# A second buffer for one weight block of every second column pair, and two of its down tiles moved to the end

## The chip, the cores and the metric

The kernel runs on one core of one Trainium2 chip. The core has a matrix engine (TensorE, PE in the rows; its weight loads are PEld), a vector engine (VectorE, DVE), an activation engine (ScalarE, ACT), GpSimd (POOL) and SyncE (SP), which only issues transfers. All five take their instructions in order and wait for one another through semaphores. The metric is the time of one execution on the device in microseconds (us), the median of several runs.

## The reference

One block of a streaming encoder on 512 positions of width 2048, all in float32: a mixer (a gated linear recurrence beside a banded attention) and then a gated feed-forward part with a causal depthwise convolution of width 3. The change touches the feed-forward part:

```
h2 = rms_norm(x, g_ffn[l])
up = causal_dwconv(h2 @ w_up[l], conv_w[l], conv_b[l])      # 2048 -> 2 * 5632
a, gate = jnp.split(up, 2, axis=-1)
x = x + (a * jax.nn.silu(gate)) @ w_down[l]                 # 5632 -> 2048
```

## The kernel before

**Up-projection.** The 11264 columns of `w_up` are taken as 44 pairs of 128 (128 columns of `a` with their 128 of the gate). The first four pairs (`lead`) are computed directly. Pairs 4 to 43, called units here, use a Strassen-Winograd scheme: the weights of a unit are four blocks of 128x1024 (512 KB each), and seven products of weight combinations with activation combinations give the result. `unit_loads` fetches what a unit needs into four buffers of the pool `ur`: `s1` (a sum of two blocks, the second added by an accumulating transfer that GpSimd issues), `a22`, `a11` and `a12`. A fifth tile, `s3`, goes into the fixed buffer `spare`. In the order of the products: `a22` (product T4), `a11` (B11), `s1` (T1), S2 = `s1`+`a11`, added in place into `a11` at L935 (T2), `a12` (B21), S4 = `a11`+`a12`, added in place into `a12` at L939 (B22), and `s3` (T3). Each is split into two float16 parts (`split16`: ACT at L880, then DVE at L881), into one of six buffers `whl`, and a product is 24 matmuls of 256 columns on these and on the split activations `thi`, `tlo`.

**Scales.** Before the first split of a unit its scale must be known: ACT takes the absolute sums of the four blocks and of the unit's down tiles (L886, into a throw-away tile `junk`), DVE and ACT make a diagonal `dg` (L770), a small matmul spreads the maximum over all partitions (L772), and DVE inverts it. One call of `period_scales` serves a unit and the down tiles that stand beside it. `m_scale` does the same for a group of four results.

**Down-projection.** It has 11 groups of four pairs with 8 weight tiles each, 88 down tiles in all, taken from `queue` in order. A down tile is a 512 KB load into one of three buffers `raw`, a split, 24 matmuls of 512 columns and two additions into the accumulators (L1063). Units 5 and 6 have three down tiles beside them, units 7 to 43 two each, unit 4 none; the last 8 tiles run in pairs after unit 43 (`plan_downs`), each pair with a scale of its own.

**Order.** `take(3)` writes out the splits up to three operands ahead of the product or down tile that consumes one; whatever a split needs first (the scale of the next unit, the loads of its down tiles) is written out there too. So with two down tiles the scale of unit j+1 is written out just before the last product T3 of unit j; with three it is written out only at the first down tile of unit j, after the code that follows T3 (the sums into `z`, the convolution taps, the gate). `unit_loads(j+1)` stands behind the addition S4 of unit j. The tile framework keeps this as a priority, moves an instruction forward when its inputs and a buffer are free, and gives a pool's buffers out in the order of the requests; so a load is issued when the tile that held its buffer has had its last reader.

**The buffers of `act`.** The pool `act` has 48 buffers of 2 KB. In `lead` it holds the 32 tiles of the split activations `hh`, `hl_`, and `t_prep(0)` to `t_prep(7)` put the 32 tiles of `thi`, `tlo` there; in the second half of `lead` each step i frees four of the former.

Of the kernel before, what the change touches and what calls it, by code (L numbers as in the profile page):

```python
# [8 lines left out]
F32 = mybir.dt.float32  # L9
# [5 lines left out]
ALU = mybir.AluOpType  # L15
PSUM = bass.MemoryType.PSUM

P = 128
T = 512
# [4 lines left out]
NPAIR_FF = 44  # L24
N_WARM = 12
NGRP = 11
N_LEAD = 4
H = 256
# [3 lines left out]
N_DOWN = N_MIX + 16 + 4 * (NPAIR_FF - N_LEAD)  # L32
# [20 lines left out]
def block_kernel(ctx: ExitStack, tc: tile.TileContext, xT, wst, cols, bias_t, masks, yT):  # L53
# [3 lines left out]
    cst = ctx.enter_context(tc.tile_pool(name="cst", bufs=1))  # L57
    wp = ctx.enter_context(tc.tile_pool(name="wp", bufs=3))
    actp = ctx.enter_context(tc.tile_pool(name="actp", bufs=48))
# [11 lines left out]
    def nm(s):  # L71
        cnt[0] += 1
        return f"{s}{cnt[0]}"
# [4 lines left out]
    def vo_t():  # L78
        return vop.tile([P, T], F32, tag="vo", name=nm("vo"))
# [7 lines left out]
    def mm_t():  # L87
        return ps_mm.tile([P, T], F32, tag="mm", name=nm("mm"))
# [4 lines left out]
    V = nc.vector  # L93
    A = nc.scalar
# [3 lines left out]
    def c3(ap, n):  # L98
        return ap.rearrange("p (a b) -> p a b", a=n)
# [25 lines left out]
    def next_w():  # L125
        while len(wq) < 1 + LOOK and wstate["prep"] < wstate["end"]:
            prep_w()
        return wq.pop(0)
# [81 lines left out]
    def rstd(r, ms):  # L210

        A.activation(r, ms, AF.Ln, bias=epst)
        A.activation(r, r, AF.Exp, scale=-0.5)
        t = wk_t()[:, :r.shape[1]]
        V.scalar_tensor_tensor(out=t, in0=ms, scalar=EPS, in1=r, op0=ALU.add, op1=ALU.mult)
        V.scalar_tensor_tensor(out=t, in0=t, scalar=-0.5, in1=r, op0=ALU.mult, op1=ALU.mult)
        V.scalar_tensor_tensor(out=r, in0=t, scalar=1.5, in1=r, op0=ALU.add, op1=ALU.mult)
# [37 lines left out]


    ssq = vo_t()
    R1 = cst.tile([P, T], F32, name="R1")
    r1c = cst.tile([P, NT], F32, name="r1c")

    def split(src):
# [14 lines left out]
    def finish_r1():  # L276
# [5 lines left out]
        rstd(r1c, ps2[:, 0:NT])  # L282
        rstd(R1, ps)

# [73 lines left out]
    def evict_r1(ps, alloc):  # L358
        x = alloc()
        V.tensor_tensor(out=x, in0=ps, in1=R1, op=ALU.mult)  # L360
        return x
# [299 lines left out]
    for blk in range(2):  # L661
# [3 lines left out]
        for h in range(4 * blk, 4 * blk + 4):  # L665
# [7 lines left out]
            g = hg_mixer(h, vt, pf, pq, pg)  # L673
            next(g)
            gens.append(g)
    for blk in range(2):
        vt = v_evict(v_gemm())
        for h in range(4 * blk, 4 * blk + 4):
# [3 lines left out]
            g = at_mixer(h, vt, pq, pk, bt)  # L682
# [4 lines left out]
    acc = [None] * KT  # L687
# [45 lines left out]
    zp = ctx.enter_context(tc.tile_pool(name="zp", bufs=1))  # L733
# [14 lines left out]

    R2 = R1

# [30 lines left out]
    gs = cst.tile([P, KT], F32, name="gs")  # L781
# [12 lines left out]
    thi, tlo = [None] * 8, [None] * 8  # L794

    def t_prep(i):
        z = zp.tile([P, 8, H], F32, tag="z", name=nm("z"))
        c2 = lambda ap: ap.rearrange("p (a b) -> p a b", a=2)
        V.scalar_tensor_tensor(out=z[:, 0:8:7, :], in0=c2(acc[i][:, :]), scalar=gs[:, i:i + 1], in1=c2(R2[:, :]), op0=ALU.mult, op1=ALU.mult)
        V.scalar_tensor_tensor(out=z[:, 1:3, :], in0=c2(acc[i + 8][:, :]), scalar=gs[:, i + 8:i + 9], in1=c2(R2[:, :]), op0=ALU.mult, op1=ALU.mult)  # L800
        b11, b21, b22, t1, t2, t3, t4, b12 = [z[:, j, :] for j in range(8)]
        V.tensor_tensor(out=t1, in0=b11, in1=b12, op=ALU.subtract)
        V.scalar_tensor_tensor(out=t2, in0=t1, scalar=-1.0, in1=b22, op0=ALU.mult, op1=ALU.subtract)
        V.tensor_tensor(out=t3, in0=b22, in1=b12, op=ALU.subtract)
        V.scalar_tensor_tensor(out=t4, in0=t2, scalar=-1.0, in1=b21, op0=ALU.mult, op1=ALU.subtract)
        hs, ls = [], []
        for o, n in ((0, 4), (4, 3)):
            h = actp.tile([P, n, H], F16, tag="act", name=nm("th"))
            l = actp.tile([P, n, H], F16, tag="act", name=nm("tl"))
            A.copy(out=h, in_=z[:, o:o + n, :])  # L810
            V.tensor_tensor(out=l, in0=z[:, o:o + n, :], in1=h, op=ALU.subtract)
            hs += [h[:, j, :] for j in range(n)]
            ls += [l[:, j, :] for j in range(n)]
        thi[i], tlo[i] = hs, ls
# [45 lines left out]
    def ur_t():  # L860
        return urp.tile([P, 1024], F32, tag="ur", name=nm("ur"))

    def raw_t():
        return wp.tile([P, 1024], F32, tag="raw", name=nm("raw"))

    def load(t, i):
        nc.sync.dma_start(out=t, in_=wst[i])
        return t

    def load_sum(t, i, k):  # L870
        nc.sync.dma_start(out=t, in_=wst[i])
        nc.gpsimd.dma_start(out=t, in_=wst[k], accum_op=ALU.add)
        return t
# [12 lines left out]
            A.activation(junk_t(), t, AF.Abs, accum_out=r[:, k:k + 1])  # L886

    units = {}

    def unit_loads(j):  # L890
        u = units.setdefault(j, {})
        i = N_MIX + 16 + 4 * (j - N_LEAD)
        u["s1"] = load_sum(ur_t(), i + 2, i + 3)
        u["a22"] = load(ur_t(), i + 3)
        u["a11"] = load(ur_t(), i)
        u["a12"] = load(ur_t(), i + 1)

    def down_loads(ds):
        return [load(raw_t(), N_DOWN + 8 * g + c2) for g, c2 in ds]

    def period_scales(j, ds):

# [63 lines left out]
    def product(ps, b):  # L966
        t = take(3)
        for k in range(8):
            cs = slice(k * P, (k + 1) * P)
            cl = slice(1024 + k * P, 1024 + (k + 1) * P)  # L970
            mm3(ps, t[:, cs], t[:, cl], thi[k][b], tlo[k][b], k == 0, k == 7)
        if later:
            later.pop(0)()

    def up_unit(j):
        bank = [mm_t() for _ in range(4)]
        z = zp.tile([P, 8, H], F32, tag="z", name=nm("z"))
        s1, u2, v = z[:, 7, :], z[:, 4, :], z[:, 5:7, :]
        two = lambda ap: ap.unsqueeze(1).broadcast_to([P, 2, H])
        b = lambda i: c3(bank[i], 2)  # L980
        product(bank[3][:, H:], T4)
        product(bank[0][:, 0:H], B11)
        A.copy(out=s1, in_=bank[0][:, 0:H])
        product(bank[2][:, 0:H], T1)
        product(bank[1][:, H:], T2)
        product(bank[1][:, 0:H], B21)
        V.tensor_tensor(out=z[:, 0:5:4, :], in0=b(1), in1=two(s1), op=ALU.add)
        product(bank[3][:, 0:H], B22)
        product(bank[2][:, H:], T3)
        V.tensor_tensor(out=v, in0=b(2), in1=two(u2), op=ALU.add)  # L990
        V.tensor_tensor(out=z[:, 1:3, :], in0=b(3), in1=v, op=ALU.add)
        V.tensor_tensor(out=z[:, 3, :], in0=bank[2][:, H:], in1=v[:, 0, :], op=ALU.add)
        cw = units.pop(j)["cw"]
        zf = z.rearrange("p a b -> p (a b)")
        ya = taps(zf[:, 0:T], j, cw[:, 0])
        yg = taps(zf[:, T:2 * T], NPAIR_FF + j, cw[:, 1])
        gated(j, ya, yg, zf[:, 0:T])
# [11 lines left out]
    def lead():  # L1009
        half = N_LEAD // 2  # L1010
        n = 0
        for j in range(half):
            u = c3(ur_t(), 2)
            for e in range(2):
                ps = mm_t()
                for h in range(2):
                    wh, wl = next_w()
                    for k in range(8):
                        cs = slice(k * P, (k + 1) * P)
                        kt = 8 * h + k  # L1020
                        mm3(ps, wh[:, cs], wl[:, cs], hh[kt], hl_[kt], kt == 0, kt == KT - 1)
                        if n == 0 and k == 3:
                            finish_r2()
                    if n % 2 == 1:
                        t_prep(n // 2)
                    n += 1
                evict_r2(ps, u[:, e])
            lead_taps(j, [u[:, 0], u[:, 1]], (ssa, rmask)[j])
        unit_loads(N_LEAD)
        pss = [mm_t() for _ in range(2 * half)]  # L1030
        for i in range(8):
            wh, wl = next_w()
            for e, kt in enumerate((i, i + 8)):
                for c in range(2 * half):
                    cs = slice((4 * e + c) * P, (4 * e + c + 1) * P)
                    mm3(pss[c], wh[:, cs], wl[:, cs], hh[kt], hl_[kt], i + e == 0, i + e == 8)
            if i % 2 == 1:
                t_prep(4 + i // 2)
            if i == 4:
                period_scales(N_LEAD, [])  # L1040
        us = [evict_r2(ps, actp.tile([P, T], F32, tag="act", name=nm("u"))) for ps in pss]
        later.extend([lambda j=j: lead_taps(half + j, us[2 * j:2 * j + 2]) for j in range(half)])
# [23 lines left out]

    mrp = ctx.enter_context(tc.tile_pool(name="mrp", bufs=2))
    steps = []
    queue = [(g, c2) for g in range(NGRP) for c2 in range(8)]
    done = 0  # L1070
    for j in range(N_LEAD, NPAIR_FF):
        steps.append(j)
        n = 0 if j == 4 else 3 if j < 7 else 2
        ds = queue[done:done + n]
        done += n
        plan_unit(j, ds)
        steps += ds
# [8 lines left out]
    for st in steps:  # L1086
# [8 lines left out]
        elif st % 4 == 3:  # L1095
            g = st // 4
# [129 lines left out]
```

## Time and profile before

| what | value |
|---|---|
| median of 3 runs | 2345.21 us (2338.12 to 2345.74) |
| the profiled execution, its own time | 2340.17 us |
| its span, first to last instruction | 2338.3 us |
| mean granted TensorE clock | 0.986 |
| TensorE matmul busy | 2210.7 us, 95% of the span |
| VectorE busy | 1672.2 us, 72% |
| ScalarE busy | 1334.9 us, 57% |
| transfers | 294.21 MB, mean 126 GB/s |

The profile is of one execution. Busy times count the engine's own instructions; matmuls are pipelined and their ends modelled. "Idle before" an instruction is time in which its engine did nothing, followed by what ended that time. The granted clock is a share of 2.4 GHz.

### The profile page before, as it was taken

What the parts mean: (1) busy time and instruction counts of PE and PEld (TensorE: products, weight loads), DVE (VectorE), ACT (ScalarE), POOL (GpSimd) and SP (SyncE); (2) the same over time, 40 slices, a digit from 0 to 9 for tenths busy, and PEclk for the clock granted to TensorE, in tenths of its full rate; (3) what the DMA queues carried; (4) which work ended last, traced back from release to release, by engine and by line L of the source; (5) the groups of instructions that cost most, each with busy time, mean ns of one, the idle gap of its engine ahead of it and who ended that gap; (6) DMA issues with size and microseconds to landing.
All of it is one profiled execution on the core that took longest, in us unless ns stands there. A gap on an engine that the chain in (4) does not pass through costs nothing.

```text
span 2338.3 us, 34658 instructions
## 1 busy us (share of the span) xinstructions
PE 2210.7 (95%) x13666; PEld 1698.5 (73%) x13666; DVE 1672.2 (72%) x2669; ACT 1334.9 (57%) x2110; POOL 271.0 (12%) x261
## 2 busy tenths in 40 slices
PE   9999999999999999986799999999999999999989
PEld 7888887888888887874467676666777676666664
DVE  7678568758568645975477877777777787777774
ACT  5455445445355334564566667666767676666652
POOL 4223123300001112000000000000000000000001
PEclk9999999999999999997899999999999999999999
DMA  6222222222323422444355555555555655555532
GB/s 206 90 73 73 90 72 81 79 93 82 99 87 97 142 99 91 142 123 128 103 160 154 150 152 148 158 154 162 154 162 154 162 153 149 152 144 158 157 100 99
DMA packets 82755, 294.21 MB, mean 126 GB/s; under 512 B 9568, under 2 KB 10208, under 8 KB 82592
## 3 DMA queue, kind: packets, MB, share of 16 engines
q1 hardware_dynamic: 68112, 240.34, 31.1%
q0 software_dynamic: 14480, 51.65, 12.0%
q8 instruction: 107, 1.75, 0.3%
q14 instruction: 56, 0.46, 0.1%
HBM read 287.76 MB, written 4.19 MB: 125 GB/s over the span
## 4 chain that ended last, share of the span: by engine, by line
PE 42%; DVE 22%; ACT 16%; DMA 14%; issue 5%; POOL 0%; SPq 0%; ACTq 0%; POOLq 0%; DVEq 0%
DMA ur<-wst 13%; PE mm L131 10%; PE mm L133 10%; PE mm L132 10%; ACT junk L886 8%; DVE whl L881 7%; ACT whl L880 3%; PE mx L131 2%; PE mx L133 2%; PE mx L132 2%; DVE vo L1063 2%; DVE vo L819 2%; ACT dg L770 1%; ACT mhl L847 1%; DVE z L990 1%
## 5 line engine op out<-in xcount | busy, mean ns | idle before, releaser
L131 PE MATMUL mm<-th,whl 128*128 128x256 f16 x2240 | 614.8, 274 | 7.3 <-ACT whl L880 7.3
L133 PE MATMUL mm<-th,whl 128*128 128x256 f16 x2240 | 614.5, 274 | 1.9 <-DVE whl L881 1.9
L132 PE MATMUL mm<-tl,whl 128*128 128x256 f16 x2240 | 614.9, 274 | 0.0
L131 PEld LDWEIGHTS <-whl 128*128 128x128 f16 x2948 | 290.2, 98 | 221.0 <-issue 104.2
L131 PE MATMUL mm<-act,whi 128*128 128x512 f32 x1024 | 406.8, 397 | 0.0
L133 PE MATMUL mm<-act,wlo 128*128 128x512 f32 x1024 | 399.8, 390 | 0.0
L132 PE MATMUL mm<-act,whi 128*128 128x512 f32 x1024 | 399.2, 390 | 0.0
L133 PEld LDWEIGHTS <-whl 128*128 128x128 f16 x2948 | 290.3, 98 | 114.3 <-issue 3.8
L132 PEld LDWEIGHTS <-whl 128*128 128x128 f16 x2948 | 290.5, 99 | 110.6 <-issue 2.7
L881 DVE SCALAR_TENSOR_TENSOR whl<-ur,sm,whl 128x1024 f16<-128x1024 f32 x240 | 305.8, 1280 | 71.8 <-ACT whl L880 71.0
L880 ACT ACTIVATE whl<-ur,sm 128x1024 f16<-128x1024 f32 x240 | 269.7, 1140 | 120.3 <-DVE uh L917 37.8
L119 ACT CAST whi<-raw 128x1024 fp32r<-128x1024 f32 (+1 forms) x161 | 167.7, 1041 | 228.5 <-PE mm L132 181.4
L122 DVE TENSOR_TENSOR wlo<-raw,whi 128x1024 fp32r<-128x1024 f32 (+1 forms) x161 | 209.6, 1303 | 92.5 <-ACT whi L119 87.7
L131 PE MATMUL mx<-mhl,whl 128*128 128x512 f16 x708 | 271.1, 383 | 0.0
L132 PE MATMUL mx<-mhl,whl 128*128 128x512 f16 x708 | 270.5, 382 | 0.0
L133 PE MATMUL mx<-mhl,whl 128*128 128x512 f16 x708 | 270.2, 382 | 0.0
L886 ACT ACTIVATE junk<-ur 128x1024 f16<-128x1024 f32 x160 | 168.1, 1051 | 169.3 <-DMA ur<-wst 169.2
L133 PEld LDWEIGHTS mm<-act,wlo 128*128 128x128 f32 x1024 | 192.3, 188 | 41.2
L131 PEld LDWEIGHTS mm<-act,whi 128*128 128x128 f32 x1024 | 192.5, 188 | 38.7 <-issue 0.5
L132 PEld LDWEIGHTS mm<-act,whi 128*128 128x128 f32 x1024 | 192.7, 188 | 38.1 <-issue 0.5
L881 DVE SCALAR_TENSOR_TENSOR whl<-raw,sm,whl 128x1024 f16<-128x1024 f32 x89 | 114.1, 1283 | 62.2 <-ACT whl L880 61.5
L1063 DVE SCALAR_TENSOR_TENSOR vo<-mx,inv,vo 128x512 f32<-128x512 f32 x177 | 131.4, 743 | 23.8 <-PE mx L133 23.6
(278 smaller groups left out, 2904.9 us busy)
## 6 DMA issues: line engine op xcount, KB each, us to landing
raw<-wst SPq DMA_DIRECT2D x248, 512.0 KB, 3.5
ur<-wst SPq DMA_DIRECT2D x160, 512.0 KB, 3.5
ur<-wst POOLq DMA_DIRECT2D x40, 512.0 KB, 5.4
spare<-wst SPq DMA_DIRECT2D x39, 512.0 KB, 4.7
spare<-wst POOLq DMA_DIRECT2D x39, 512.0 KB, 7.8
vo<-xT SPq DMA_DIRECT2D x16, 256.0 KB, 4.7
vo<-xT POOLq DMA_DIRECT2D x16, 256.0 KB, 3.1
yT<-vo POOLq DMA_DIRECT2D x13, 256.0 KB, 2.3
```

The costliest lines, as they stand in the source:

```text
L119: A.copy(out=hi[:, c], in_=raw[:, c])
L122: V.tensor_tensor(out=lo[:, c], in0=raw[:, c], in1=hi[:, c].bitcast(F32), op=ALU.subtract)
L131: PE.matmul(ps, lhsT=sh, rhs=mh, start=start, stop=False)
L132: PE.matmul(ps, lhsT=sh, rhs=ml, start=False, stop=False)
L133: PE.matmul(ps, lhsT=sl, rhs=mh, start=False, stop=stop)
L770: A.activation(dg[:, i], ident, AF.Copy, scale=t[:, i:i + 1])
L819: V.scalar_tensor_tensor(out=y[:, 1:], in0=u[:, :T - 1], scalar=cw[:, 1:2], in1=y[:, 1:], op0=ALU.mult, op1=ALU.add)
L847: A.activation(t[:, :T], ms[j], AF.Copy, scale=m[:, 2:3])
L880: A.activation(t[:, 0:1024], x, AF.Copy, scale=s)
L881: V.scalar_tensor_tensor(out=t[:, 1024:], in0=x, scalar=s, in1=t[:, 0:1024], op0=ALU.mult, op1=ALU.subtract)
L886: A.activation(junk_t(), t, AF.Abs, accum_out=r[:, k:k + 1])
L1063: V.scalar_tensor_tensor(out=acc[c][:, ts_], in0=ps[:, ts_], scalar=inv, in1=acc[c][:, ts_], op0=ALU.mult, op1=ALU.add)
```

## The change

- `R1` (also `R2`), a fixed tile of 512 columns, becomes the first half of a fixed tile `spare2` of 1024 columns. Odd units load `a12` there in place of a buffer of `ur`; the rest of the four `ur` buffers serve as before.
- `z` shrinks from eight blocks of 256 columns to six. The two others come from `act`: `x` (t4, b12) in `t_prep`, `su` (s1, u2) in `up_unit`. Three wide instructions of `t_prep` and one of `up_unit` are cut in two for that.
- `t_prep` moves later: numbers 0 to 2 stand behind lead steps n = 2, 4, 6 (before: 1, 3, 5, 7 for 0 to 3), numbers 3 to 7 behind steps i = 1, 2, 4, 6, 7 of the second half (before: 1, 3, 5, 7 for 4 to 7).
- Units 5 to 43 have two down tiles each, 78 in all (before: 80), and ten run at the end. Of these, tiles 1, 2, 5, 6, 9 and 10 load into `ur` buffers, the others into `raw`.

```diff
-    R1 = cst.tile([P, T], F32, name="R1")
+    spare2 = cst.tile([P, 2 * T], F32, name="spare2")
+    R1 = spare2[:, 0:T]
...
     def t_prep(i):
-        z = zp.tile([P, 8, H], F32, tag="z", name=nm("z"))
+        z = zp.tile([P, 6, H], F32, tag="z", name=nm("z"))
+        x = actp.tile([P, 2, H], F32, tag="act", name=nm("x"))
...
-        V.scalar_tensor_tensor(out=z[:, 0:8:7, :], in0=c2(acc[i][:, :]), scalar=gs[:, i:i + 1], in1=c2(R2[:, :]), op0=ALU.mult, op1=ALU.mult)
+        for e, o in ((0, z[:, 0, :]), (1, x[:, 1, :])):
+            c = slice(e * H, (e + 1) * H)
+            V.scalar_tensor_tensor(out=o, in0=acc[i][:, c], scalar=gs[:, i:i + 1], in1=R2[:, c], op0=ALU.mult, op1=ALU.mult)
...
-        for o, n in ((0, 4), (4, 3)):
+        for n, srcs in ((4, [z[:, 0:4, :]]), (3, [z[:, 4:6, :], x[:, 0:1, :]])):
...
+    DOWNS = [(g, c2) for g in range(NGRP) for c2 in range(8)]
+    N_BESIDE = 2 * (NPAIR_FF - N_LEAD - 1)
...
-        u["a12"] = load(ur_t(), i + 1)
+        u["a12"] = load(spare2 if j % 2 else ur_t(), i + 1)
 
     def down_loads(ds):
-        return [load(raw_t(), N_DOWN + 8 * g + c2) for g, c2 in ds]
+        at_end = DOWNS.index(ds[0]) - N_BESIDE
+        new = ur_t if at_end >= 0 and at_end % 4 == 0 else raw_t
+        return [load(new(), N_DOWN + 8 * g + c2) for g, c2 in ds]
...
     def up_unit(j):
         bank = [mm_t() for _ in range(4)]
-        z = zp.tile([P, 8, H], F32, tag="z", name=nm("z"))
-        s1, u2, v = z[:, 7, :], z[:, 4, :], z[:, 5:7, :]
+        z = zp.tile([P, 6, H], F32, tag="z", name=nm("z"))
+        su = actp.tile([P, 2, H], F32, tag="act", name=nm("su"))
+        s1, u2, v = su[:, 0, :], su[:, 1, :], z[:, 4:6, :]
...
-        V.tensor_tensor(out=z[:, 0:5:4, :], in0=b(1), in1=two(s1), op=ALU.add)
+        V.tensor_tensor(out=u2, in0=bank[1][:, H:], in1=s1, op=ALU.add)
+        V.tensor_tensor(out=z[:, 0, :], in0=bank[1][:, 0:H], in1=s1, op=ALU.add)
...
-                    if n % 2 == 1:
-                        t_prep(n // 2)
+                    if n in (2, 4, 6):
+                        t_prep(n // 2 - 1)
...
-            if i % 2 == 1:
-                t_prep(4 + i // 2)
+            if i in (1, 2, 4, 6, 7):
+                t_prep((0, 3, 4, 0, 5, 0, 6, 7)[i])
...
-        n = 0 if j == 4 else 3 if j < 7 else 2
+        n = 0 if j == N_LEAD else 2
```

## Rows read from the trace of the kernel before

**Rows 1.** The page: busy time, share of the span, instructions of each engine.
```profile
PE 2210.7 (95%) x13666; PEld 1698.5 (73%) x13666; DVE 1672.2 (72%) x2669; ACT 1334.9 (57%) x2110; POOL 271.0 (12%) x261
```
**Rows 2.** TensorE's waits, whole span: us in total, times, longest.
```profile
PE mx L772 <- ACT dg L770: 97.1, 41, 14.4
```
**Rows 3.** Windows: length; PE, PEld, DVE, ACT, POOL busy; PEclk; DMA share, GB/s.
```profile
1010.40:1028.74 18.34, 18.34 (x169) 16.43 (x169) 13.03 (x19) 13.48 (x24) 0.00 (x0) 1.00 0.43 136
1167.16:1177.51 10.35, 10.35 (x50) 4.70 (x48) 10.35 (x15) 5.96 (x8) 0.87 (x1) 1.00 0.48 112
1031.10:1164.40 133.30, 93.22 (x628) 63.55 (x628) 75.29 (x109) 66.05 (x99) 6.08 (x7) 0.83 0.42 117
1196.08:2238.20 1042.12, 989.74 (x7380) 724.01 (x7380) 797.31 (x1168) 706.10 (x1060) 59.35 (x68) 1.00 0.57 155
```
**Rows 4.** Timeline of TensorE, scale matmuls: start, us, instruction, idle before and releaser.
```profile
1078.84 0.37 PE L772 MATMUL mx<-dg,on1b 128*128 128x256 bf16 x1 [14.39 <-ACT dg L770]
...
1128.86 0.37 PE L772 MATMUL mx<-dg,on1b 128*128 128x256 bf16 x1 [13.35 <-ACT dg L770]
...
1164.43 0.27 PE L772 MATMUL mx<-dg,on1b 128*128 128x256 bf16 x1 [2.62 <-ACT dg L770]
...
1196.08 0.27 PE L772 MATMUL mx<-dg,on1b 128*128 128x256 bf16 x1 [1.97 <-ACT dg L770]
...
2279.56 0.27 PE L772 MATMUL mx<-dg,on1b 128*128 128x128 bf16 x1 [9.67 <-ACT dg L770]
```
**Rows 5.** Timeline of ScalarE around the end of unit 5.
```profile
1057.85 1.15 ACT L880 ACTIVATE whl<-spare,sm 128x1024 f16<-128x1024 f32 x1 [6.71 <-DMA spare<-wst]
...
1065.94 1.52 ACT L818 ACTIVATE vo<-z,colt,cw 128x512 f32<-128x512 f32 x2 [5.91 <-DVE z L991]
...
1070.19 1.04 ACT L886 ACTIVATE junk<-ur 128x1024 f16<-128x1024 f32 x1
...
1077.04 1.04 ACT L886 ACTIVATE junk<-raw 128x1024 f16<-128x1024 f32 x1
```
**Rows 6.** The chain that ended last, before the scale matmul at 1531.10.
```profile
1522.57 4.60 DMA ur<-wst
...
1527.20 3.23 ACT junk L886 x6
```
**Rows 7.** Timeline of SyncE's queue in the same unit.
```profile
1515.38 5.06 SPq L867 DMA_DIRECT2D ur<-wst  x2
...
1522.57 0.33 SPq L867 DMA_DIRECT2D ur<-wst  x1
1523.88 3.59 SPq L867 DMA_DIRECT2D raw<-wst  x2
```
**Rows 8.** Tile raw, the one load issued between 1523.5 and 1524.5.
```profile
DMA to landing us min/median/max: 5.1/5.1/5.1
```
**Rows 9.** Tile raw, the one load issued between 1526.9 and 1527.5.
```profile
DMA to landing us min/median/max: 7.2/7.2/7.2
```
**Rows 10.** The page: loads of raw, times, KB each, median us to landing.
```profile
raw<-wst SPq DMA_DIRECT2D x248, 512.0 KB, 3.5
```
**Rows 11.** Timeline of ScalarE in a unit that also splits four results (mhl).
```profile
1552.24 2.56 ACT L847 ACTIVATE mhl<-m,mg 128x512 f16<-128x512 f32 x4 [0.18 <-DVE mg L841]
...
1555.74 1.04 ACT L886 ACTIVATE junk<-ur 128x1024 f16<-128x1024 f32 x1
```
**Rows 12.** Tile z, whole span: duration ns min/median/max, first and last start, forms.
```profile
L987 DVE TENSOR_TENSOR z<-mm,z x40: 679/681/692, 1023.7 to 2265.0; 128x512 f32<-128x512 f32 x40
...
L992 DVE TENSOR_TENSOR z<-mm,z x40: 413/416/420, 1032.4 to 2272.9; 128x256 f32<-128x256 f32 x40
```
**Rows 13.** Timeline of VectorE at the end of lead: last t_prep, first split.
```profile
988.62 0.75 DVE L799 SCALAR_TENSOR_TENSOR z<-vo,gs,R 128x512 f32<-128x512 f32 x1
...
992.94 2.09 DVE L811 TENSOR_TENSOR tl<-z,th 128x1024 f16<-128x1024 f32 x2
...
1000.68 1.28 DVE L881 SCALAR_TENSOR_TENSOR whl<-ur,sm,whl 128x1024 f16<-128x1024 f32 x1 [4.00 <-ACT whl L880]
```

More of the change, by code (lines that the diff above doesn't have):

```diff
@@ L796, in t_prep @@
     def t_prep(i):
-        z = zp.tile([P, 8, H], F32, tag="z", name=nm("z"))
+        z = zp.tile([P, 6, H], F32, tag="z", name=nm("z"))
+        x = actp.tile([P, 2, H], F32, tag="act", name=nm("x"))
         c2 = lambda ap: ap.rearrange("p (a b) -> p a b", a=2)
-        V.scalar_tensor_tensor(out=z[:, 0:8:7, :], in0=c2(acc[i][:, :]), scalar=gs[:, i:i + 1], in1=c2(R2[:, :]), op0=ALU.mult, op1=ALU.mult)
+        for e, o in ((0, z[:, 0, :]), (1, x[:, 1, :])):
+            c = slice(e * H, (e + 1) * H)
+            V.scalar_tensor_tensor(out=o, in0=acc[i][:, c], scalar=gs[:, i:i + 1], in1=R2[:, c], op0=ALU.mult, op1=ALU.mult)
         V.scalar_tensor_tensor(out=z[:, 1:3, :], in0=c2(acc[i + 8][:, :]), scalar=gs[:, i + 8:i + 9], in1=c2(R2[:, :]), op0=ALU.mult, op1=ALU.mult)
-        b11, b21, b22, t1, t2, t3, t4, b12 = [z[:, j, :] for j in range(8)]
+        b11, b21, b22, t1, t2, t3 = [z[:, j, :] for j in range(6)]
+        t4, b12 = x[:, 0, :], x[:, 1, :]
         V.tensor_tensor(out=t1, in0=b11, in1=b12, op=ALU.subtract)
@@ L806, in t_prep @@
         hs, ls = [], []
-        for o, n in ((0, 4), (4, 3)):
+        for n, srcs in ((4, [z[:, 0:4, :]]), (3, [z[:, 4:6, :], x[:, 0:1, :]])):
             h = actp.tile([P, n, H], F16, tag="act", name=nm("th"))
             l = actp.tile([P, n, H], F16, tag="act", name=nm("tl"))
-            A.copy(out=h, in_=z[:, o:o + n, :])
-            V.tensor_tensor(out=l, in0=z[:, o:o + n, :], in1=h, op=ALU.subtract)
+            j = 0
+            for src in srcs:
+                o = slice(j, j + src.shape[1])
+                j += src.shape[1]
+                A.copy(out=h[:, o], in_=src)
+                V.tensor_tensor(out=l[:, o], in0=src, in1=h[:, o], op=ALU.subtract)
             hs += [h[:, j, :] for j in range(n)]
@@ L1068, in block_kernel @@
     steps = []
-    queue = [(g, c2) for g in range(NGRP) for c2 in range(8)]
+    queue = DOWNS
     done = 0
```

## Prediction, made before the changed kernel was run

> **What bounds the kernel now.** I read the page first: TensorE is busy for 95% of the span [rows 1], so only its idle time and its slow clock can be won. Then its waits: one line holds nearly all of them in the feed-forward part, the small matmul L772 that spreads a scale, which waited 97.1 us in 41 places for ScalarE's `dg` [rows 2]. Then the windows, for what TensorE needs when nothing stops it: seven products take 18.34 us, 2.62 each, and two down tiles 10.35, 5.18 each [rows 3]. The third window holds units 5 to 7, between the scale matmuls of units 5 and 8: 133.3 us at a granted clock of 0.83. By the matmuls in it that is 20 products and 6 down tiles, 52.4 + 31.1 = 83.5 us of work; 49.8 us are lost. The fourth holds 34 later units: 1042.1 us with 989.7 busy, so 52.4 us idle, 1.54 a unit [rows 3]. Last the timeline of the scale matmuls [rows 4]: 14.39 us in front of the one for unit 6, 13.35 for unit 7, then 2.62, then 1.97 and the like, and 9.67 near the end. So there are three places: the first units, the steady loop, the end.
>
> **First units: three down tiles become two.** With three, the scale of unit 6 is written out behind the tail of unit 5. ScalarE shows it: it waits 5.91 us for the sums into `z`, does the taps, and only then starts the absolute sums at 1070.19, the last at 1077.04 [rows 5]; TensorE stands until 1078.84 with the down tiles of unit 5 queued behind the scale. With two, the scale is written out before T3, ahead of that tail, as in every later unit. The new stretch from scale 5 to scale 8 holds 20 products and 4 down tiles: 52.4 + 20.7 = 73.1 us. What stays lost: unit 5's own start. Its T3 waits for `s3`, whose split begins at 1057.85 after 6.71 us of waiting for the load and takes 1.15 [rows 5], so T3 begins 27.9 us after 1031.1 where six products need 15.7: 12.2 us, which I keep whole. For the scales of units 6, 7 and 8 I take 1, 2.6 and 2.6 us, the last two from the wait of 2.62 at 1164.43 [rows 4]. Sum 73.1 + 12.2 + 6.2 = 91.5, against 133.3: **41.8 us won**. One absolute sum fewer before the scale of unit 5 gives another 1.0 [rows 5]. The bound below: if the new waits at scales 6 to 8 are 5 us each, 33; above, if unit 5's start also mends by half, 48.
>
> **The end: ten tiles instead of eight.** Two down tiles more on a TensorE that has nothing beside them: **10.35 us lost** [rows 3]. The stall of 9.67 us there belongs to the scale of the last group of results, in front of the two tiles beside unit 43 [rows 4]; the code that puts it there is not touched, so I leave it: from 0 to 9.67 us of gain. The new `ur` buffers of the end change no wait of TensorE that I can see; their cover is the 10.35 us that each pair of tiles gives to the loads behind it.
>
> **The steady loop: `a12`.** The chain of one unit shows what is late: the load of `a12` is issued at 1522.57, when the split of S4 has freed its buffer, takes 4.60 us, and the three last absolute sums (1.08 us each) stand behind it, 3.23 us, up to `dg` and L772 at 1531.10 [rows 6]. After the change the seven `ur` tiles of two units rotate through four buffers. An odd unit's `a12` has `spare2`, free since the split of S4 two units earlier; an even unit's `s1` takes the buffer that was spared, and its `a22`, `a11` and `a12` each move one release forward, so `a12` waits for the addition S4, like `a11` now, which SyncE issues some 2.4 us sooner (second load of the pair that begins at 1515.38) [rows 7]. What is late next: the unit's second down tile, in a `raw` buffer that the split of the first down tile before it frees. It is issued at 1523.88 [rows 7] and lands 5.1 us later, at 1528.98 [rows 8], where its sum starts at 1527.20 + 2 x 1.08 = 1529.36 now. So with an unmoved `raw` load a unit wins 0.38 us; with a `raw` load at the median of 3.5 us [rows 10] it would be 1.95, more than the mean wait. In 8 of the 34 units, those that also split four results, the scale waits 1.97 us and the loads have landed: the sums run from 1555.74 without a stop behind the splits of ScalarE [rows 11], and an earlier load changes nothing. Left are 52.4 - 8 x 1.97 = 36.6 us in 26 units, 1.41 each. I take 0.85, about the middle between 0.38 and 1.41, since the load at 1522.57 goes but another of its size, the early one of the next unit, may be issued in its place: **22 us won**, bounds 10 and 36.6 (52.4 if the order on ScalarE changes as well).
>
> Here a rule of the Trainium skill speaks against the change. The `raw` load lands after 5.1 us and its successor, issued 3.3 us later beside an accumulating transfer, after 7.2 [rows 8, 9], against a median of 3.5 [rows 10]: loads that run together slow each other down. The page "DMA: Bandwidth & Descriptors", section "Issuing engines are not separate DMA queues", says that transfers of all queues run on the same 16 engines and interleave, so issuing one elsewhere or earlier buys no bandwidth; by it the early load takes from the `raw` load what the late one took, and the steady loop would win no more than 0.38 us a unit, or lose.
>
> **The rest.** One addition of 512 columns becomes two of 256: 2 x 0.416 - 0.681 = 0.15 us a unit on VectorE [rows 12]. VectorE is busy 797 of 1042 us in the steady window [rows 3] and hides it; uncovered, it would be 40 x 0.15 = 6 us. `t_prep` gets one more cut instruction on VectorE in the scaling and one more split on each of VectorE and ScalarE, some 0.5 us for each of eight. It also needs one more `act` buffer, so the last one waits for one more step of `lead`, 24 matmuls of 512 columns like a down tile, 5.2 us or a little more: from 988.62 to about 994. It ran until 995.0 and VectorE then stood 4.00 us before the split at 1000.68 [rows 13]. It would now end near 1002, the first splits of unit 4 move back by up to 2 us, and the first product at 1010.40 [rows 3] still finds its operands 5 us old or more. Queued behind on VectorE are those splits; TensorE would wait for them only with 7 us more. I count nothing; with the cover gone it is up to 5. `su` brings `act` to at most 32 + 8 results and their splits + 1, which leaves 7 of 48 for six `junk`: no wait. The first `a12` in `spare2` waits for the last reader of `R2`, in `lead`, which is done before unit 4 starts; SyncE's loads behind it lose nothing.
>
> **Sum.** 41.8 + 1.0 - 10.35 + 22 = 54.5 us off the profiled execution's own time of 2340.2 us gives 2285.7; its time lies 5 us under the median of the runs shown (2345.2) and 2 above the lowest, so I say 2287.
>
> **The rivals.**
> 1. The steady loop wins nothing, for the `raw` load is as late as before and its slack is used up; only the first units win: 2340.2 - 32.5 = 2308. For it: rows 8. Against: the three sums behind `a12` would no longer all be late.
> 2. The steady loop loses all its waits, because the `raw` load lands sooner and ScalarE's order closes up: 2340.2 - 32.5 - 52.4 = 2255. For it: 36.6 us hang on one load. Against: the 8 units whose loads are early now and wait all the same [rows 11].
> 3. The early stall does not go: the scale of unit 6 is still placed behind the tail. Then units 5 to 7 win only their two tiles, 10.35, which the end takes back, and the steady 22 stay: 2318. Against: all 37 units with two tiles have it in front.
> 4. Slower: the early loads (an odd unit's `a12`, an even unit's `s1` with its accumulation) are issued around 1522 to 1524, beside `s3` and the `raw` load that the scale needs, and this one lands after 7.2 us as its successor does now [rows 9], not 5.1. Beyond the slack of 0.38 each unit then waits 1.7 us more; 36 x 1.7 = 62 against 32.5 won: 2370. It decides from a landing 1.3 us later than now (0.38 + 32.5/36). By the skill's rule above the time would lie between rivals 1 and 4. Against: one load of that size leaves the stretch for each that comes.
>
> **Chances.** Forecast 0.50, rival 1 0.20, rival 2 0.16, rival 3 0.06, rival 4 0.06, others 0.02. The range 2258 to 2313 holds the forecast (2265 to 2306 by its own bounds), rival 1 and half of rival 2. 0.3% of the time, 7 us, is about what a measurement can tell from no change. Forecast and rivals 1 to 3 are faster: 0.92; same 0.02; slower 0.06.
>
> **What the changed profile would show.** Right: the scale matmuls of units 6 and 7 wait under 4 us, and ScalarE's absolute sums stand before the taps of unit 5; the stretch from scale 5 to scale 8 takes about 91 us; units run at 29.8 us in the mean, with the last absolute sum waiting for a `raw` load and not an `ur` one; from the scale of unit 43 to the end it is 10 us longer. Wrong: a wait over 5 us at scale 6 or 7 (rival 3), landings of `raw` over 6 us with waits over 2 at each scale (rival 4), a wait for `t_prep` at the first product.

## Result and the profile after

The changed kernel takes 2280.8 us (median of 4 runs, 2279.0 to 2283.8), the kernel before 2345.5 in the same session (4 runs, 2338.1 to 2349.0): ratio 0.9729, 95% interval 0.9703 to 0.9756. The forecast was 2287, in a range of 2258 to 2313.

The page's busy line and TensorE's waits over the whole span (line, what it waited for, us in total, times, longest), to hold against [rows 1, 2]; L773 is the old L772:

```profile
PE 2200.5 (97%) x13667; PEld 1694.6 (74%) x13667; DVE 1672.4 (73%) x2729; ACT 1336.8 (59%) x2119; POOL 271.3 (12%) x261
```
```profile
PE mx L773 <- ACT dg L771: 46.8, 34, 9.7
```

The scale matmul still heads the list of waits, with half the time: 46.8 us against 97.1. The matmul busy time fell by 10.2 us; the number of matmuls is the same but for one. Windows of the same stretches as in [rows 3] (length; busy PE, PEld, DVE, ACT, POOL; granted clock; DMA share, GB/s): from the scale of unit 5 to the start of its T3, from there to the scale of unit 8, 34 later units, and from the scale of unit 43 to the end:

```profile
1030.57:1057.90 27.33, 19.45 (x147) 15.16 (x146) 19.44 (x32) 17.69 (x27) 0.87 (x1) 0.88 0.47 134
1057.90:1121.31 63.41, 59.81 (x435) 43.11 (x436) 48.70 (x72) 45.07 (x69) 4.36 (x5) 0.97 0.62 167
...
1153.23:2167.46 1014.23, 983.65 (x7379) 721.35 (x7379) 798.07 (x1202) 707.97 (x1060) 58.58 (x67) 1.00 0.58 159
2167.46:2277.30 109.84, 96.58 (x547) 53.80 (x546) 65.29 (x114) 41.96 (x61) 7.10 (x13) 0.95 0.24 83
```

The scale matmuls of units 5 to 9 and of the last group, in TensorE's timeline, against [rows 4]:

```profile
1030.57 0.27 PE L773 MATMUL mx<-dg,on1b 128*128 128x256 bf16 x1 [1.52 <-ACT dg L771]
1063.26 0.27 PE L773 MATMUL mx<-dg,on1b 128*128 128x256 bf16 x1 [0.25 <-ACT dg L771]
1091.72 0.27 PE L773 MATMUL mx<-dg,on1b 128*128 128x256 bf16 x1 [1.78 <-ACT dg L771]
1121.31 0.27 PE L773 MATMUL mx<-dg,on1b 128*128 128x256 bf16 x1 [0.62 <-ACT dg L771]
1153.23 0.27 PE L773 MATMUL mx<-dg,on1b 128*128 128x256 bf16 x1 [2.02 <-ACT dg L771]
...
2208.77 0.27 PE L773 MATMUL mx<-dg,on1b 128*128 128x128 bf16 x1 [9.67 <-ACT dg L771]
```

The two waits of 14.39 and 13.35 us are gone; the 9.67 near the end is unchanged. Between the same scale matmuls of both profiled executions:

| stretch | before, us | after, us | won | forecast |
|---|---|---|---|---|
| start to scale 5 | 1031.1 | 1030.6 | 0.5 | 1.0 |
| scale 5 to scale 8 | 133.3 | 90.7 | 42.6 | 41.8 |
| scale 8 to scale 9 | 31.7 | 31.9 | -0.3 | 0 |
| scale 9 to scale 43 (34 units) | 1042.2 | 1014.2 | 27.9 | 22 |
| scale 43 to the end | 100.0 | 109.8 | -9.8 | -10.35 |
| span | 2338.3 | 2277.3 | 61.0 | 54.5 |

In the 34 units the idle time in front of the scale matmuls fell from 52.4 to 30.6 us, 21.8 of the 27.9. The other 6.1 are TensorE's busy time, 989.74 before and 983.65 after for the same matmuls. Most of it is the granted clock. Before, it stood at 0.50 (the level of 1.2 GHz) in three stretches of the 34 units, 10.2 us together, and at half the clock these do the work of 5.1 us. Each begins right behind a scale matmul that had waited 1.97 us (units 9, 13 and 29). The changed kernel's profile has no such stretch there, though its scale of unit 9 waits 2.02 us. The windows behind that scale, first before, then after:

```profile
1196.60:1200.00 3.40, 3.40 (x17) 2.29 (x16) 2.10 (x7) 2.69 (x4) 0.00 (x0) 0.50 0.03 7
```
```profile
1153.60:1157.00 3.40, 3.40 (x25) 2.21 (x23) 2.54 (x7) 2.54 (x4) 0.00 (x0) 1.00 0.71 146
```

### The profile page after: what moved, and what is told of

It reads as the page before. It is cut to its first block, busy times and chain, and to the rows that moved or that the text cites. A ratio compares the mean times of both kernels' runs of the same rounds, so it can differ in the third digit from the quotient of the medians.

```text
span 2277.3 us, 34675 instructions
## 1 busy us (share of the span) xinstructions
PE 2200.5 (97%) x13667; PEld 1694.6 (74%) x13667; DVE 1672.4 (73%) x2729; ACT 1336.8 (59%) x2119; POOL 271.3 (12%) x261
## 4 chain that ended last, share of the span: by engine, by line
PE 49%; DVE 28%; ACT 11%; issue 6%; DMA 6%; POOL 0%; SPq 0%; ACTq 0%; DVEq 0%; POOLq 0%
PE mm L131 12%; PE mm L133 12%; PE mm L132 12%; DVE whl L890 8%; DMA raw<-wst 5%; ACT junk L895 4%; ACT whl L889 4%; DVE vo L1078 3%; PE mx L133 3%; PE mx L131 3%; PE mx L132 3%; DVE vo L828 2%; DVE vo L829 2%; DVE ur L948 1%; ACT dg L771 1%
## 5 line engine op out<-in xcount | busy, mean ns | idle before, releaser
L889 ACT ACTIVATE whl<-ur,sm 128x1024 f16<-128x1024 f32 x206 | 231.1, 1142 | 154.2 <-DVE ur L948 52.1
L119 ACT CAST whi<-raw 128x1024 fp32r<-128x1024 f32 (+1 forms) x161 | 167.7, 1042 | 228.9 <-PE mm L132 183.7
L890 DVE SCALAR_TENSOR_TENSOR whl<-ur,sm,whl 128x1024 f16<-128x1024 f32 x206 | 261.4, 1277 | 41.0 <-ACT whl L889 41.0
L131 PEld LDWEIGHTS mm<-act,whi 128*128 128x128 f32 x1024 | 192.4, 188 | 38.8 <-issue 0.5
L895 ACT ACTIVATE junk<-ur 128x1024 f16<-128x1024 f32 x146 | 152.1, 1044 | 0.0
L890 DVE SCALAR_TENSOR_TENSOR whl<-raw,sm,whl 128x1024 f16<-128x1024 f32 x83 | 106.3, 1283 | 43.1 <-ACT whl L889 42.2
```

Source lines behind the costliest of these rows:

```text
L119: A.copy(out=hi[:, c], in_=raw[:, c])
L131: PE.matmul(ps, lhsT=sh, rhs=mh, start=start, stop=False)
L889: A.activation(t[:, 0:1024], x, AF.Copy, scale=s)
L890: V.scalar_tensor_tensor(out=t[:, 1024:], in0=x, scalar=s, in1=t[:, 0:1024], op0=ALU.mult, op1=ALU.subtract)
```

## The experiments

In all of them the times are medians, with the ratio to the kernel before on the same chip. The column of waits in the table at the end of this section is the idle time in front of the scale matmuls of the 34 units, summed from the timeline.

**1. The kernel before with two down tiles beside units 5 and 6, nothing else.**

```diff
-        n = 0 if j == 4 else 3 if j < 7 else 2
+        n = 0 if j == 4 else 2
```

> The kernel before with one edit: two down tiles beside units 5 and 6, ten at the end, all in raw. Theory (the order with three tiles puts the scale behind the tail of the unit): the waits in front of the scales of units 6 and 7 fall from 14.4 and 13.4 us to under 4 each, the stretch from scale 5 to scale 8 from 133 to about 91 us, the end grows by 10, the 34 later units stay at 1042 us within 5: 2345 - 32 = 2313 us. Rival (a good part of the first units' gain comes with the second buffer): the stretch stays over 100 us and the time over 2322.

2312.1 us (2308.2 to 2315.0), ratio 0.9879 (0.9861 to 0.9896). The waits at the scales of units 6, 7 and 8 are 0.25, 4.36 and 0.00; the stretch from scale 5 to scale 8 takes 93.4 us, the steady loop 1041.9 as before, the end 111.0. So the number of tiles alone wins the early stretch and pays the end.

**2. Three tiles kept, but the scale of units 6 and 7 written out one operand sooner**, so that it stands in front of T3 and ahead of the tail.

```diff
-    def product(ps, b):
-        t = take(3)
+    def product(ps, b, ahead=3):
+        t = take(ahead)
...
-        product(bank[2][:, H:], T3)
+        product(bank[2][:, H:], T3, 4 if j in (5, 6) else 3)
```

> The kernel before with one edit: three tiles stay beside units 5 and 6, but at their last product T3 the operands are written out four ahead and not three, so the next scale is written out ahead of the unit's tail. Theory (order): the two waits of 27.7 us together fall under 12, the time to 2318 to 2330. Rival (three tiles in three raw buffers: each load waits for a split of the unit before, whatever the order): together they stay over 20 us, the time within 6 us of 2345.

2317.9 us (2314.0 to 2320.2), 0.9903 (0.9887 to 0.9919). The two waits are 4.42 and 7.33 us, 11.75 together instead of 27.7. The place of the scale in the order set most of the stall; with three tiles a remainder stays that two tiles don't have. The 34 later units, whose code is that of the kernel before, wait 45.4 us instead of 52.4: so much differs between two profiles of the same loop. Since nothing is added at the end (99.1 us), the whole comes within 6 us of experiment 1.

**3. The changed kernel without the second buffer for `a12`.**

```diff
-        u["a12"] = load(spare2 if j % 2 else ur_t(), i + 1)
+        u["a12"] = load(ur_t(), i + 1)
```

> The changed kernel with one part undone: a12 always in a buffer of ur. Theory (the steady gain of 28 us is the earlier load): the 34 units go back from 1014 to about 1042 us, a unit's last absolute sum of an ur block waits for its load again, the time is about 2281 + 28 = 2309. Rival (the smaller z and su, which free the next unit's sums from waiting for the old z, gave it): within 4 us of 2281.

2301.5 us (2297.5 to 2304.7), 0.9834 (0.9816 to 0.9851). The steady loop takes 1034.8 us, not the expected 1042: its waits are 43.6, neither 30.6 nor 52.4. The buffer is not the whole gain. The other 8.8 us of waits are only 1.8 under the 45.4 of experiment 2, so the waits alone don't show that another edit took them; experiment 4 looks for it.

**4. Experiment 1 with `su` in the pool `act` and the wide addition cut in two**, no second buffer, `z` left at eight blocks.

```diff
-        s1, u2, v = z[:, 7, :], z[:, 4, :], z[:, 5:7, :]
+        su = actp.tile([P, 2, H], F32, tag="act", name=nm("su"))
+        s1, u2, v = su[:, 0, :], su[:, 1, :], z[:, 4:6, :]
...
-        V.tensor_tensor(out=z[:, 0:5:4, :], in0=b(1), in1=two(s1), op=ALU.add)
+        V.tensor_tensor(out=u2, in0=bank[1][:, H:], in1=s1, op=ALU.add)
+        V.tensor_tensor(out=z[:, 0, :], in0=bank[1][:, 0:H], in1=s1, op=ALU.add)
```

> The kernel of the first experiment (two tiles beside each unit, a12 in ur) with one more edit: s1 and u2 of a unit in act buffers and the one addition cut in two. Without a second buffer for a12 the changed kernel had its 34 units in 1035 us, the first experiment in 1042. Theory (these two tiles in act let the sums of a unit start while z is still read): the 34 units come to about 1035. Rival (it is the order the framework happens to choose, or the cut t_prep): they stay at 1042, or gain nothing by 2 us.

2305.0 us (2303.3 to 2308.8), 0.9837 (0.9815 to 0.9859). The time and the steady stretch of 1038.2 us (1041.9 in experiment 1, 1034.8 in experiment 3) settle little by themselves, and the waits, 42.0 us against 51.3 in experiment 1, not much more, since experiment 2 has 45.4 with the loop of experiment 1. The time as a whole is lower than in experiment 1 by its ratio (0.9837 against 0.9879, the intervals just apart). What differs beyond doubt is ScalarE's order. The line of the absolute sums that wait for an `ur` load, over the 34 units, first in the kernel before, then here (line, what it waited for, us in total, times, longest):

```profile
ACT junk L886 <- DMA ur<-wst: 161.3, 97, 3.9
```
```profile
ACT junk L886 <- DMA ur<-wst: 30.4, 26, 1.8
```

Before, ScalarE's order mixes the sums with the splits, as its timeline shows in the unit of [rows 6]:

```profile
1514.79 1.06 ACT L886 ACTIVATE junk<-ur 128x1024 f16<-128x1024 f32 x1 [3.00 <-DMA ur<-wst]
...
1516.45 1.14 ACT L880 ACTIVATE whl<-ur,sm 128x1024 f16<-128x1024 f32 x1
...
1518.80 1.06 ACT L886 ACTIVATE junk<-ur 128x1024 f16<-128x1024 f32 x1 [0.17 <-DMA ur<-wst]
...
1520.08 1.15 ACT L880 ACTIVATE whl<-ur,sm 128x1024 f16<-128x1024 f32 x1
...
1521.38 1.15 ACT L880 ACTIVATE whl<-raw,sm 128x1024 f16<-128x1024 f32 x1
1523.61 1.06 ACT L886 ACTIVATE junk<-ur 128x1024 f16<-128x1024 f32 x1 [1.08 <-DMA ur<-wst]
...
1524.66 1.13 ACT L880 ACTIVATE whl<-raw,sm 128x1024 f16<-128x1024 f32 x1
1527.20 1.06 ACT L886 ACTIVATE junk<-ur 128x1024 f16<-128x1024 f32 x1 [1.40 <-DMA ur<-wst]
```

Two sums, at 1514.79 and 1518.80, wait for their loads in front of the splits of S2 (1516.45) and S4 (1520.08); the one at 1523.61 waits with a `raw` split behind it. Here both splits stand in front of the first sum:

```profile
1473.26 1.15 ACT L880 ACTIVATE whl<-ur,sm 128x1024 f16<-128x1024 f32 x1 [1.07 <-DVE ur L935]
...
1477.45 1.15 ACT L880 ACTIVATE whl<-ur,sm 128x1024 f16<-128x1024 f32 x1 [1.19 <-DVE ur L939]
...
1479.81 1.04 ACT L886 ACTIVATE junk<-ur 128x1024 f16<-128x1024 f32 x1
```

So it is throughout: in the kernel before and in experiments 1 and 2, 52 sums in 26 of the 34 units stand in front of the split of S4, in experiments 3 and 4 and in the changed kernel none. ScalarE meets 26 late loads instead of 97 (29.5 us of waits in 26 places in experiment 3). Its idle time as a whole fell only from 336.1 to 329.7 us; it now waits elsewhere. Why the framework orders them so when `su` is apart wasn't tried.

**5. The changed kernel with the ten end tiles all in `raw`.**

```diff
-        new = ur_t if at_end >= 0 and at_end % 4 == 0 else raw_t
+        new = raw_t
```

> The changed kernel with one part undone: the ten tiles of the end all load into raw, none into ur. Theory (TensorE's 10.4 us for each pair cover those loads): within 3 us of 2281, no wait of TensorE in the last 60 us but the 9.7 us of the last group's scale. Rival (three raw buffers are too few for ten tiles): waits at the scales of the pairs, 4 to 15 us slower.

2284.0 us (2282.4 to 2285.0), 0.9760 (0.9744 to 0.9776). The end takes 110.7 us against 109.8, so the `ur` slots are worth some 1 us there. The steady loop, whose code is that of the changed kernel, shows 27.4 us of waits but 990.6 of matmul busy time against 983.7. The clock accounts for it: it stood at 0.50 in four stretches of the loop, 13.7 us together, which costs 6.8 of the 6.9 us. Each lies behind a scale matmul that had waited 2.0 us; the changed kernel's profile has the same waits and no such stretch. So two profiles of one loop differ by as much as the 6.1 us that the waits leave over in the result.

**6. The changed kernel with a pool of four `raw` buffers** (its memory from `act`, 46 buffers instead of 48).

```diff
+    rawp = ctx.enter_context(tc.tile_pool(name="rawp", bufs=4))
-    actp = ctx.enter_context(tc.tile_pool(name="actp", bufs=48))
+    actp = ctx.enter_context(tc.tile_pool(name="actp", bufs=46))
...
-        return wp.tile([P, 1024], F32, tag="raw", name=nm("raw"))
+        return rawp.tile([P, 1024], F32, tag="raw", name=nm("raw"))
```

> The changed kernel with a fourth raw buffer, paid for with two of the 48 act buffers. Theory (what the 26 ordinary units still wait for is their second down tile, whose buffer comes free too late): ScalarE's waits for raw fall from 12.9 us in the steady part to near nothing and the 34 units from 1014 to about 1003 us: 0.4 to 0.5% under the changed kernel. Rival (the 16 engines are shared, so an earlier issue only moves the crowd): the loads land later after issue, the 34 units stay within 3 us of 1014.

2261.4 us (2261.2 to 2267.5), 0.9655 (0.9635 to 0.9675). The waits at the scales of ordinary units are gone: 17.0 us are left in the 34 units, 16.1 of them in the 8 units that split a group of results. ScalarE waits for no `raw` load any more. The stretch from scale 5 to scale 8 wins too, 84.8 us against 90.7.

**7. The sums of the next unit's `s1` and `a22` written out early, behind the split of `s3`.**

```diff
+            v = units.get(j + 1)
+            if v is not None and "s1" in v:
+                v["early"] = sm_t()
+                abs_sums(v["early"][:, 0:2], [v[n] for n in ("s1", "a22")])
```

> The changed kernel with the absolute sums of s1 and a22 of the next unit written out behind the split of s3 and not at the next unit's scale. Theory (in the 8 units that also split four results the scale waits only for the order of six sums on ScalarE, their loads having landed): their waits fall from 2.0 us each to under 1, the 34 units from 1014 to 1000 to 1008 us. Rival (VectorE or the splits set that time, not ScalarE's order, or ScalarE now stands at loads not yet landed): the 2.0 us stay, or the ordinary units lose what these win; 1011 us or more.

2315.4 us (2308.6 to 2316.5), 0.9873 (0.9852 to 0.9894), slower than the changed kernel. The 8 group units keep 2.02 us each; the others wait 38.8 us instead of 14.5, and ScalarE's waits for `raw` are 35.5 us in 26 places against 14.1 in 19. The 34 units take 1053.2 us, 38.9 more than in the changed kernel: 24.3 by waits, the rest by matmul busy time, for the clock stood at 0.50 for 30.7 us of them. The theory fell.

**8. The changed kernel with the last group's scale and splits written out behind the two tiles beside unit 43.**

```diff
         if isinstance(st, tuple):
+            if st == DOWNS[N_BESIDE]:
+                while later:
+                    later.pop(0)()
             down(*st)
             continue
...
-        if st == NPAIR_FF - 1:
-            while later:
-                later.pop(0)()
```

> The changed kernel with the scale of the last group written out behind the two tiles beside unit 43 and not ahead of them. Theory (the wait of 9.7 us stands only because that scale is ahead of two tiles that need nothing of it): the wait goes, the first tiles run at full clock, 10 to 12 us less from the scale of unit 43 to the end. Rival (the tail of unit 43 and the last four splits are the true bound, for the tiles of the last group come at once): the wait moves behind the two tiles; under 4 us won.

2279.2 us (2275.9 to 2286.3), 0.9729 (0.9704 to 0.9754): no change. TensorE's timeline of the scale matmuls there:

```profile
2208.31 0.27 PE L773 MATMUL mx<-dg,on1b 128*128 128x128 bf16 x1 [5.70 <-ACT dg L771]
2223.50 0.22 PE L773 MATMUL mx<-dg,on1b 128*128 128x128 bf16 x1 [2.38 <-ACT dg L771]
```

One wait of 9.67 us became two of 8.08 together: the scale of the next pair of tiles stands behind the same tail of unit 43 on ScalarE. The end takes 108.3 us instead of 109.8, which is too little to show in the time.

**9. The four splits of a group (`mhl`) one unit later.** Seven empty entries go ahead of them in the list from which each product takes one.

```diff
             g = st // 4
+            if st < NPAIR_FF - 1:
+                later.extend([lambda: None] * 7)
             later.append(lambda g=g: (m_scale(g), m_split(4 * g)))
```

> The changed kernel with the four result splits (mhl) of a group, and the scale before them, written out one unit later, behind the first four products of the unit after. Theory: in the 8 units that split a group the wait of 2.0 us at the scale comes from ScalarE's order, since the 2.56 us of mhl run in front of the last sums; without them there the eight waits go from 2.0 to about 0 and the stretch from scale 9 to scale 43 takes 1014.2 - 16 = 998 us, the time about 2264. Rival: another chain of fixed length (the silu, the gate and the scale's own path) sets the 2.0 us, or the four splits only move to another unit's sums; then the eight waits stay or come back in the next unit, and the time stays at 2277 to 2283.

2279.3 us (2275.7 to 2282.9), 0.9748 (0.9731 to 0.9764): as the changed kernel. The wait went with the splits. The scale matmul of unit 9 has no idle time, that of unit 10, where the splits now stand, has 1.87; the 8 group scales wait 1.7 us in all instead of 16.1, the units after them about 1.9 each:

```profile
1149.31 0.27 PE L773 MATMUL mx<-dg,on1b 128*128 128x256 bf16 x1
...
1181.08 0.27 PE L773 MATMUL mx<-dg,on1b 128*128 128x256 bf16 x1 [1.87 <-ACT dg L771]
```

So the splits in front of the sums cause these waits, as the theory said; that the wait would vanish was wrong, as the rival said.

**10. Experiments 6 and 9 together.**

> The changed kernel with a pool of its own of four raw buffers (act 46) and the result splits one unit later. Theory: the two causes of waits are separate, ordinary units by the raw load and group units by ScalarE's order, so both go: steady stretch 1003.3 - 16 = 987 us and the time about 2245. Rival: where the splits only move, the time stays near 2260, that of the kernel with four raw buffers alone; where 46 act buffers are too few with results held a unit longer, it is above 2265.

2257.3 us (2256.4 to 2258.3), 0.9649 (0.9634 to 0.9663); experiment 6's interval covers it. The units with the splits wait 1.9 us, all others at most 0.15.

**11. Four `raw` buffers, and all four splits behind T3**, after the next unit's scale.

```diff
+            if st < NPAIR_FF - 1:
+                later.extend([lambda: None] * 6)
-            later.append(lambda g=g: (m_scale(g), m_split(4 * g)))
-            later.extend([lambda j=j: m_split(j) for j in range(4 * g + 1, 4 * g + 4)])
+            later.append(lambda g=g: (m_scale(g), [m_split(j) for j in range(4 * g, 4 * g + 4)]))
```

> The changed kernel with four raw buffers of their own (act 46) and all four result splits of a group written out together behind the product T3 that follows the next unit's scale, so that on ScalarE they stand behind that unit's last absolute sums and before most of the splits of the unit after. Theory: the wait follows the splits' place: 2.56 us of ScalarE between two scales where ScalarE's order has no slack; put at the start of the stretch they run in idle time that ScalarE has there, so the eight waits of 2.0 us (1.9 in the kernel that only moved them a unit later) go below 0.5, the stretch from scale 9 to scale 43 takes about 987 us and the time is about 2245. Rival: any 2.6 us more in a unit delays that unit's sums, wherever they stand; then 1.5 to 2 us stay in eight units and the time stays at 2256 to 2260. If the splits delay T4 or a down tile instead, new idle time stands there and the time is above 2260.

2249.8 us (2246.0 to 2250.5), 0.9601 (0.9576 to 0.9625): 31 us under the changed kernel and the fastest of all. ScalarE's timeline shows the last sum and the scale of unit 9, the splits 7 us behind it, and TensorE's scale matmuls of units 9 and 10:

```profile
1143.69 1.04 ACT L896 ACTIVATE junk<-raw 128x1024 f16<-128x1024 f32 x1
...
1144.73 0.72 ACT L772 ACTIVATE dg<-ident,sm 128x128 bf16<-128x128 f32 x2
...
1152.83 2.54 ACT L857 ACTIVATE mhl<-m,mg 128x512 f16<-128x512 f32 x4
```
```profile
1145.65 0.27 PE L774 MATMUL mx<-dg,on1b 128*128 128x256 bf16 x1
...
1175.46 0.27 PE L774 MATMUL mx<-dg,on1b 128*128 128x256 bf16 x1 [0.68 <-ACT dg L772]
```

The same 2.54 us of ScalarE cost TensorE 0.7 to 1.5 us in each such unit instead of 2.0; the expected 0.5 wasn't reached. The 34 units have 8.1 us of waits left:

```profile
1145.70:2136.00 990.30, 982.22 (x7389) 721.52 (x7387) 800.81 (x1211) 709.65 (x1065) 58.68 (x67) 1.00 0.59 163
```

| kernel | 34 units, us | waits in them, us | time, us | ratio |
|---|---|---|---|---|
| before (first session) | 1042.2 | 52.4 | 2345.5 | 1 |
| 1: two tiles | 1041.9 | 51.3 | 2312.1 | 0.9879 |
| 4: two tiles, `su` | 1038.2 | 42.0 | 2305.0 | 0.9837 |
| 3: changed, no second buffer | 1034.8 | 43.6 | 2301.5 | 0.9834 |
| changed | 1014.2 | 30.6 | 2280.8 | 0.9729 |
| 6: four `raw` | 1003.3 | 17.0 | 2261.4 | 0.9655 |
| 11: four `raw`, splits behind T3 | 990.4 | 8.1 | 2249.8 | 0.9601 |

## Why the prediction was right, and which terms were mis-sized

**First units: right.** Forecast 41.8 us won, 42.6 measured, and the mechanism is the forecast one: the absolute sums of unit 6 run at 1058.8 to 1062.4, behind the splits and ahead of unit 5's taps, and experiments 1 and 2 show that both the number of tiles and the place of the scale do it. Inside the stretch two parts are off and cancel. T3 of unit 5 starts 27.4 us after the scale (forecast 27.9). From there on, the waits at scales 6 to 8 are 0.25 + 1.78 + 0.62 = 2.65 us, forecast 6.2; but 63.41 us pass, where 63.6 were forecast with all work at full speed. About half of that difference is the clock, which stood at 0.50 for 3.4 us from 1059.8; the rest lies in small gaps and slower matmuls. The 1.0 us for the scale of unit 5 came out at half: the stretch ahead of it is 0.5 us shorter, its wait 1.52 instead of 2.19. Rival 3 is refuted by the wait of 0.25.

**The end: right.** 9.8 us against 10.35, and the stall of 9.67 stayed. Experiment 8 shows that moving the one scale that stands behind it doesn't remove it.

**The steady loop: the sum of waits right, its cause half right.** The forecast was 22 us for the second buffer and nothing for the cuts around `z`. The waits fell by 21.8, but in two parts, and that these add up to the forecast is luck. With the code of the kernel before, the loop waits 52.4, 51.3 and 45.4 us (before, experiments 1 and 2); with `su` and without the buffer 43.6 and 42.0 (3 and 4); with both 30.6, 27.4 and 28.1 (the changed kernel, 5 and 8). So the buffer took away 11 to 16 us of waits, 13.0 by the two kernels that differ in it alone (43.6 - 30.6), and `su` with its addition 2 to 10, 9.3 by its pair (51.3 - 42.0). The term for `a12` was mis-sized, 13 for 22 and still within its bounds of 10 to 36.6, and the step that failed is that the edits around `su` were counted as nothing ("hides it", "no wait"). I had weighed them by VectorE's 0.15 us and by the buffers of `act`; what they changed is ScalarE's order, which I had left as a condition of the upper bound only ("52.4 if the order on ScalarE changes as well"). That the worth of `su` came through this order is likely but not shown: no run changes the order alone.

The sum left a third part out. The 6.1 us of matmul busy time are nearly all of what the span won beyond the forecast (61.0 against 54.5). 5.1 of them come from the clock of the profiled executions, and they can't be put down to an edit: experiment 5 runs the changed kernel's loop with 6.9 us more. By time, the buffer is worth 17.4 us against experiment 5 of the same session (2301.5 - 2284.0), and 2301.5 - 2280.8 = 20.7 across two sessions, more than its 13.0 us of waits.

**What is late next: right.** The chain that ended last shows it in two successive ordinary units (start, us, what; x2 is one sum and the reading of its accumulator), to hold against [rows 6]:

```profile
1533.19 5.98 DMA raw<-wst
1539.20 1.15 ACT junk L895 x2
...
1563.06 5.73 DMA raw<-wst
1568.82 1.15 ACT junk L895 x2
```

One sum stands behind the last load where there were three. SyncE's queue in the first of these units shows the early load of the odd unit's `a12` into the second buffer just ahead of the `raw` load, as feared in rival 4:

```profile
1531.89 0.33 SPq L876 DMA_DIRECT2D spare<-wst  x1
1533.19 2.41 SPq L876 DMA_DIRECT2D raw<-wst  x2
```

(The second buffer, like the first, goes by the name of the tile `spare` in these rows.) Landings of `raw` over the 34 units, before and after:

```profile
DMA to landing us min/median/max: 4.3/5.6/9.3
```
```profile
DMA to landing us min/median/max: 4.7/5.8/9.4
```

The median is 0.2 us later, where rival 4 needed 1.3: it didn't come about. The reason given against it, that one late load goes for each that comes, fits this but was not tested by itself. Experiment 6 is the proof from the other side: with the `raw` load a buffer earlier the ordinary waits vanish, 14.5 to 0.9 us. Rival 1 (no gain in the loop) is refuted by the waits, rival 2 (no waits left) by the same 30.6; it names what experiment 11 nearly reaches.

**The rule weighed in the prediction.** The Trainium skill's page "DMA: Bandwidth & Descriptors", section "Issuing engines are not separate DMA queues", says that transfers issued by ScalarE, SyncE or GpSimd run on the same 16 DMA engines and interleave. That an earlier issue buys no bandwidth is what the prediction drew from it; the page itself speaks of issuing from several engines. The landings of `raw` agree: they did not become shorter (5.6 and 5.8 us). What the prediction made of it for the time, at most 0.38 us a unit, didn't come true: the waits fell by 13.0 us over 26 ordinary units, 0.5 each, by the buffer, and by 13.6 more when `raw` was issued earlier. The loads take as long as before but start earlier and run beside work.

**The 8 group units: right.** They were forecast to keep 1.97 us each and keep 2.01 to 2.02. Experiments 9 and 11 show what I had read from [rows 11]: 2.56 us of splits in front of the sums.

**The rest.** The cover for `t_prep` held: the last one's scaling starts at 992.26 instead of 988.62 (about 994 was forecast), and VectorE still waits 1.94 us before the first split of unit 4, at 1000.92. The sign "29.8 us in the mean" had taken 0.85 us off every unit and not off 26 of 34; 22 us over all 34 give 30.0. That 29.8 was measured is owed to the clock: 5.1 us over 34 units are 0.15 each.

## What to carry to other kernels

Where an in-order engine mixes work that waits for loads with work that feeds the bottleneck, price an edit by what it does to that order, not by its instructions: moving two small tiles to another pool and cutting one addition changed ScalarE's order in 26 of 34 units and went with 2 to 10 us less waits, and moving 2.5 us of splits from one side of the sums to the other won some 10. One profile of a loop gives its waits to some 7 us here, so a smaller difference wants several kernels with the same loop. A buffer pays for the load that is last; when it has moved that load forward, look which is last then and give that one the next buffer. A stall whose scale is written behind a long tail shrinks when the scale is written ahead of the tail (27.7 to 11.75 us in experiment 2); moving the one waiting instruction back handed the wait to the next that stands behind the same tail (9.67 to 8.08 us in experiment 8).

## What the chip showed that was not expected

A wait of TensorE can cost more than its own length. The same matmuls of 34 units were busy for 982 to 998 us in thirteen profiles. In nine of them the granted clock stood at 0.50 for part of that time, from 3.4 us in experiment 8 to 30.7 in experiment 7; with half of this time taken off, all thirteen lie between 981 and 985. Of the 38 such stretches, 34 follow a group unit's scale matmul that had waited 2.0 us, the other four lie in or behind longer waits, of 2.7 to 4.2 us. But most waits of 2.0 us have none behind them: the changed kernel has eight in these units, and none of these stretches.

Longer landings cost the path little: in experiment 11 the `raw` loads of the 34 units landed after 6.9 us in the median, 1.3 us later than in the kernel before (5.6), and that kernel is the fastest.

```profile
DMA to landing us min/median/max: 4.7/6.9/8.7
```
